# A hybrid decoder layer on one core: stores moved to SyncE's queue, taps and branch pieces traced later

## The chip, the cores and the metric

The kernel runs on one core of a Trainium2 chip. The metric is the time of one execution on the device in microseconds (us), the median of several runs. A core has TensorE (PE in the profile; PEld is its weight load), VectorE (DVE), ScalarE (ACT), GpSimd (POOL) and SyncE (SP). SP, ACT and POOL can each issue DMA transfers; each takes its own instructions, the issues among them, in order, and an instruction that waits holds up what stands behind it on that engine.

## The reference, cut to what matters

One layer over 256 tokens of width 2048, all in float32:

```python
h = rmsnorm(x, pre_norm_g)
q_a, c_kv, k_rope, z_mla, c_in, b_gate, c_gate, z_conv, g_mla, g_conv = split(h @ w_in)
q  = rmsnorm(q_a, q_a_norm_g) @ w_q_b             # 16 heads of 128 + 64 (rotary)
kv = rmsnorm(c_kv, kv_a_norm_g) @ w_kv_b          # 16 heads, keys 128 and values 128
attn = softmax(causal(q k^T * scale)) v * silu(z_mla)
y_mla  = attn @ w_o_mla                            # 2048 x 2048
u = c_gate * c_in
conv = sum(conv_w[k] * shift(u, 2 - k) for k in range(3))
y_conv = (b_gate * conv * silu(z_conv)) @ w_o_conv # 2048 x 2048
merged = sigmoid(g_mla) * y_mla + sigmoid(g_conv) * y_conv
out = x + rmsnorm(merged @ w_out, post_norm_g)
```

## The kernel before

**A product.** PE works in fp32r. Each float32 operand is split into a high part (an ACT copy, `hi`, line 263) and a low part (a DVE subtraction, `lo`, line 264), and a product is three matmuls: high by high, low by high, high by low. Weights come from memory in units of 2048 columns by 128 rows (1 MB): a `raw` tile (three buffers, loaded by SP in `load_raw`, line 165), split by halves into `whi` and `wlo` (five buffers of 1024 columns each). `plan` lists the units in order; `ahead` loads up to three units ahead of use and splits one ahead. A quarter of a 2048 x 2048 product (four blocks of 128 rows, two token halves t = 0 and 1, each into its own PSUM bank) is 24 matmuls of 512 columns. The helper `products` first runs the 16 matmuls with `whi` for both banks and then the 8 with `wlo`; the helper `product` runs the three matmuls of one block one after the other.

**The heads stage** (up to about 608 us). After the two latents, a loop over 16 heads h runs four quarters each, `channels(h, 0..3)`, into two banks `cv` that the next head uses again (one of the four channel projections c_gate, c_in, b_gate, z_conv for a block of 512 columns per head, so four heads make one block of the convolution branch). `channels_done` reads the banks out: ACT lines 804 and 808, DVE lines 806 and 812. At every fourth head four quarters of `gates` (z_mla, banks `z`) come first, with the values of four heads (`group_v`, whose banks `vv` share the tag of `cv`). Between the quarters stand the heads' own small matmuls: `qn`, `kn`, `qr`, scores (`sc`, `sw`), values (`o`). Transposes go over memory: DVE transposes 32 x 32 blocks (line 356), POOL stores (`far<-via`, line 364) and loads them back (line 368).

**Taps.** `taps(j, t)` makes the convolution: POOL brings shifted copies of u into `mv` (line 830) and the filter rows into `cw`, DVE multiplies and adds (line 846). It is a generator in three parts, advanced by `next(tap)` at chosen places of the loop.

**Forms.** The gates g_mla and g_conv are computed by a Strassen-like scheme in seven half-size products, whose left operands are sums of quarters of x, the `FORMS`. `make_forms` builds 14 parts of them in the heads stage (ACT line 894, DVE line 896), two buffers, and POOL stores each to memory (`far_form`, line 901) when the generator is next advanced; SP loads the whole form back later (`bring_form`, line 924).

**The paired stage** (about 608 to 967 us). A sequence `seq` of steps, each with load, split, matmuls and something to run after: four sets s0 to s3 of the scheme (steps Q1, V5, V6, V7, V3, V4, Q2, banks sX, sZ, sY, weights `b`, `first_rt`, `first_rb`, `first_rc`) with the quarters of the two branch products between them (p: attention, four blocks, operand `at_both`; v: convolution, operand `cv_both`; banks `sq`). Splits are traced when the step two places earlier runs. Two of the additions of weights in a set are made by the transfer itself (`add_by_transfer`, POOL, line 1241). `turned_unit` loads transposed operands into a raw buffer and splits them. In s0 and s1 `weigh` multiplies a branch block with its gate and `keep` stores it (`kept_m`, POOL, line 1135). In s2 and s3 `merge` takes it back (`fetch`, line 1138, two buffers `y`), adds the other branch, transposes the sum by DVE and stores it by four POOL transfers (`far_m`, line 364). `later(n, fn)` runs fn n steps later.

**The out stage** (from 967 us). w_out in 16 units, operand `m_both` loaded from `far_m` by POOL; then norm, residual `xr` (2 MB, loaded on ACT's queue, line 1521) and stores.

Instructions marked `keep_in_program_order` stay in the order of tracing on their engine: all matmuls, nearly all DMA issues named here, SP's loads from `u_first` on. Others, most splits and the raw loads of the heads stage among them, are put in order at build time by a planner with a model of the times.

## Time and profile before

| | |
|---|---|
| median of 3 runs | 1063.7 us (1063.62 to 1066.05) |
| the profiled execution's own time | 1066.4 us |
| its span, first to last instruction | 1064.6 us |
| PE busy | 1018.1 us, 4552 matmuls |
| DVE, ACT, POOL busy | 793.2, 579.6, 201.0 us |
| mean granted TensorE clock | 0.984 |

A row of the timeline reads: start, duration, engine, line, operation, tiles written and read, shapes, count, and in brackets the idle time of the engine just before and what ended it. A row of the waits reads: engine, tile and line that waited, the engine and instruction waited for, microseconds in total, number of times, the longest. A row of groups ends with busy time, mean duration and idle time with its releasers.

### The profile page before, as it was taken

To read this page: it belongs to the slowest core of one execution; us is meant where nothing else is said; L and a number is where in the kernel's file an instruction comes from. 1 tells how busy PE (TensorE), PEld (TensorE's weight loads), DVE (VectorE), ACT (ScalarE), POOL (GpSimd) and SP (SyncE) were. 2 spreads that over 40 slices of the span, in tenths; PEclk is the share of its full clock that TensorE was granted. 3 is DMA by queue.
4 is the path that set the end of the run, shared out by engine and by line. 5 is a ranking of instruction groups with operands and counts; after the bars stand their busy time and mean duration, and the time that the engine had idled before them with its cause. 6 is when DMAs were issued, how large, how long until landed. Compare 5 with 4: busy or idle time off the path is not lost.

```text
span 1064.6 us, 13052 instructions
## 1 busy us (share of the span) xinstructions
PE 1018.1 (96%) x4552; PEld 839.3 (79%) x4552; DVE 793.2 (75%) x1087; ACT 579.6 (54%) x824; POOL 201.0 (19%) x362
## 2 busy tenths in 40 slices
PE   9999999999899999999999976999999999799997
PEld 7888788887688778788788755888788788588786
DVE  7588878778667796767868486788788789586562
ACT  7675545655446555455555443664665665473451
POOL 4610322203411223212233120001010013102100
PEclk9999999999899999999999988999999999899999
DMA  9776777768777675856677979989889885949652
GB/s 358 288 239 227 268 241 261 253 207 299 240 274 237 222 269 197 273 201 224 242 255 273 325 259 352 342 309 256 262 324 300 267 322 172 256 185 363 233 187 79
DMA packets 52882, 275.22 MB, mean 259 GB/s; under 512 B 8880, under 2 KB 11568, under 8 KB 26960
## 3 DMA queue, kind: packets, MB, share of 16 engines
q1 hardware_dynamic: 35280, 213.30, 54.8%
q0 software_dynamic: 17104, 57.80, 19.6%
q10 hardware_dynamic: 432, 3.29, 0.8%
q8 instruction: 35, 0.57, 0.2%
q14 instruction: 31, 0.25, 0.1%
HBM read 246.07 MB, written 24.12 MB: 254 GB/s over the span
## 4 chain that ended last, share of the span: by engine, by line
PE 72%; DMA 14%; DVE 7%; ACT 3%; issue 3%; POOL 1%; DVEq 0%; ACTq 0%; SPq 0%; POOLq 0%
PE cv L88 22%; PE sq L88 15%; PE sX L88 7%; PE out L88 6%; PE z L88 6%; PE sZ L88 4%; DMA raw<-wcv_dram 3%; DVE wlo L264 3%; DMA raw<-wsq_dram 2%; PE qa L88 2%; PE sY L88 2%; PE ckv L88 2%; DMA cw<-cwr_dram 2%; DMA far_form<-form 2%; PE kn L88 2%
## 5 line engine op out<-in xcount | busy, mean ns | idle before, releaser
L263 ACT ACTIVATE whi<-raw 128x1024 fp32r<-128x1024 f32 (+1 forms) x302 | 301.0, 1024 | 276.5 <-PE cv L88 95.7
L264 DVE TENSOR_TENSOR wlo<-raw,whi 128x1024 fp32r<-128x1024 f32 (+1 forms) x300 | 350.4, 1189 | 119.9 <-ACT whi L263 52.3
L88 PE MATMUL cv<-whi,x_both 128*128 128x512 f32 x1024 | 246.0, 393 | 7.9 <-ACT cv_f L804 4.3
L88 PEld LDWEIGHTS cv<-whi,x_both 128*128 128x128 f32 x1024 | 191.5, 189 | 51.2 <-ACT cv_f L804 6.0
L88 PE MATMUL cv<-wlo,x_both 128*128 128x512 f32 x512 | 126.4, 389 | 0.0
L88 PEld LDWEIGHTS cv<-wlo,x_both 128*128 128x128 f32 x512 | 96.1, 188 | 19.9
L264 DVE TENSOR_TENSOR slo_V<-b,shi_V 128x1024 fp32r<-128x1024 f32 x60 | 71.5, 1221 | 29.9 <-PE sq L88 14.5
L263 ACT ACTIVATE shi_V<-b 128x1024 fp32r<-128x1024 f32 x60 | 61.5, 1053 | 53.7 <-PE sq L88 34.4
L88 PE MATMUL sq<-whi,at_both 128*128 128x512 f32 x256 | 64.9, 408 | 11.2 <-ACT whi L263 11.2
L364 POOL DMA_DIRECT2D far<-via x64 | 35.3, 557 | 193.5 <-DVE via L356 191.0
L88 PEld LDWEIGHTS sq<-whi,at_both 128*128 128x128 f32 x256 | 50.8, 200 | 23.0 <-ACT whi L263 12.0
L88 PE MATMUL z<-whi,x_both 128*128 128x512 f32 x256 | 60.7, 389 | 0.0
L88 PE MATMUL sq<-whi,cv_both 128*128 128x512 f32 x256 | 60.6, 389 | 0.0
L88 PE MATMUL sX<-shi_V,form 128*128 128x512 f32 x192 | 49.4, 401 | 8.7 <-ACT sb L1282 8.7
L88 PEld LDWEIGHTS sq<-whi,cv_both 128*128 128x128 f32 x256 | 48.1, 188 | 10.0
L88 PEld LDWEIGHTS z<-whi,x_both 128*128 128x128 f32 x256 | 47.8, 188 | 9.9 <-ACT at_f L535 0.2
L88 PE MATMUL out<-whi,m_both 128*128 128x512 f32 x208 | 49.8, 390 | 2.2 <-ACT m_both L263 1.4
L88 PEld LDWEIGHTS sX<-shi_V,form 128*128 128x128 f32 x192 | 36.9, 193 | 17.7 <-ACT sb L1282 10.0
L88 PEld LDWEIGHTS out<-whi,m_both 128*128 128x128 f32 x208 | 39.0, 188 | 11.0 <-ACT m_both L263 1.8
L264 DVE TENSOR_TENSOR slo_Q<-b,shi_Q 128x1024 fp32r<-128x1024 f32 x28 | 33.6, 1221 | 5.4 <-PE sq L88 3.2
L263 ACT ACTIVATE shi_Q<-b 128x1024 fp32r<-128x1024 f32 x28 | 28.7, 1053 | 15.4 <-PE sq L88 7.5
L88 PE MATMUL sq<-wlo,at_both 128*128 128x512 f32 x128 | 32.2, 391 | 0.7 <-DVE wlo L264 0.7
(304 smaller groups left out, 1552.0 us busy)
## 6 DMA issues: line engine op xcount, KB each, us to landing
raw<-wcv_dram SPq DMA_DIRECT2D x64, 1024.0 KB, 5.9
raw<-wsq_dram SPq DMA_DIRECT2D x48, 1024.0 KB, 6.3
b<-wsq_dram SPq DMA_DIRECT2D x26, 1024.0 KB, 8.7
raw<-wz_dram SPq DMA_DIRECT2D x16, 1024.0 KB, 4.9
b<-wsq_dram POOLq DMA_DIRECT2D x12, 1024.0 KB, 11.7
raw<-wqk_dram SPq DMA_DIRECT2D x8, 1024.0 KB, 6.8
far_form<-form POOLq DMA_DIRECT2D x14, 512.0 KB, 8.6
form<-far_form SPq DMA_DIRECT2D x7, 1024.0 KB, 14.4
```

What stands on the lines that cost most here:

```text
L88: return tc.keep_in_program_order(nc.tensor.matmul(*a, **kw))
L263: a = nc.scalar.activation(hi, src, AF.Copy)
L264: b = nc.vector.tensor_tensor(lo, src, hi.bitcast(F32), op=ALU.subtract)
L364: tc.keep_in_program_order(queue.dma_start(out=f[i], in_=m))
```

## The change

- `far_form` (14 stores), `kept_m` (8) and `far_m` (32 in 8 blocks) are issued by SP instead of POOL. In `weigh` and `merge` the store, and in `merge` the next fetch, is traced one step later (`later(1, ...)`); if the block that a merge needs is not on its way, it is fetched at once. Of s3 the last two blocks are fetched at V7 into an area of their own instead of through the two `y` buffers.
- `quarter` (all 80 quarters of the heads stage) uses `product` per block, bank t = 0 first and then bank t = 1.
- At heads 4, 8 and 12 the taps' second part moves from the second to the fourth quarter of `gates`, the third part from before `gates_done` to after `channels(h, 0)`.
- The weights `first_rt` of s0's first step are fetched by SP at quarters 0 and 2 of head 14, form 11 at head 15 instead of 14.
- Each `turned_unit` is split by blocks, one step per block; the first unit of `at` moves from the end of head 15 into s0 behind Q1; the others are spread likewise.
- `xr` is issued by SP, in order behind the raw loads traced before it.

```diff
@@ load_raw
+        elif i in u_first:
+            pieces = []
@@ quarter
-        products([
-            (pss[t][:, :], [x_both[:, k, o + t * P : o + (t + 1) * P] for o in (0, S)], w(k - 4 * i, 512), k == 0, k == KD - 1)
-            for t in range(NT) for k in range(4 * i, 4 * i + 4)
-        ])
+        for t in range(NT):
+            for k4 in range(4):
+                k = 4 * i + k4
+                a = [x_both[:, k, o + t * P : o + (t + 1) * P] for o in (0, S)]
+                product(pss[t][:, :], a, w(k4, 512), k == 0, k == KD - 1)
@@ channels
+        if h == H - 2 and i in (0, 2):
+            u = u_first[i // 2]
+            tc.keep_in_program_order(nc.sync.dma_start(out=early[u][:, :], in_=plan[u][0]))
         if i == 3:
             if h == H - 1:
-                at_u[0][0]()
                 ahead(u_first[0])
-                at_u[0][1]()
@@ make_forms
-                    nc.gpsimd.dma_start(
+                    nc.sync.dma_start(
@@ turned_unit
-        return [load, split, None, None]
+        return [[load if i == 0 else None, split(i), None, None] for i in range(len(far))]
@@ the loop over heads
                 elif v and i == 1:
                     pt = turn(ps_by_head.pop(h - 1))
-                    next(tap)
...
+                elif v and i == 3:
+                    next(tap)
-            if v:
-                next(tap)
-            else:
+            if not v:
                 latent_split("ckv", ckv, "kv_g")
...
         channels(h, 0)
+        if v and at == 0:
+            next(tap)
...
-        if h == H - 2:
+        if h == H - 1:
             bring_form("11")
@@ keep
-        queue = nc.gpsimd if key[0] == "m" else nc.scalar
-        tc.keep_in_program_order(queue.dma_start(out=kept[key][:, :], in_=t[:, :]))
+        tc.keep_in_program_order(nc.sync.dma_start(out=kept[key][:, :], in_=t[:, :]))
@@ weigh
-        keep(("m", c, t), g)
+        later(1, lambda: keep(("m", c, t), g))
@@ merge
+        if (c, t) not in fetched:
+            fetch()
...
-        go, _ = turned(m[:, :], g[:, :], 4, far_m[c][:, 512 * t : 512 * (t + 1)])
-        go()
-        fetch()
+        go, _ = turned(m[:, :], g[:, :], 4, far_m[c][:, 512 * t : 512 * (t + 1)], nc.sync)
+        later(1, go)
+        later(1, fetch)
@@ the sequence
-        "Q1": p[0][:2], "V5": at_u[1:2] + p[0][2:3] + at_u[2:3] + p[0][3:],
+        "Q1": at_u[:1] + p[0][:1] + at_u[1:2] + p[0][1:2], "V5": at_u[2:3] + p[0][2:3] + at_u[3:] + p[0][3:],
...
-    also(s3["V6"][1], lambda: first_fetches([(2, 1), (2, 0), (3, 0), (3, 1)]))
+    also(s3["V6"][1], lambda: first_fetches([(2, 1), (2, 0)]))
+    def last_fetches():
+        area = spool.tile([P, UNIT], F32, name="m3_area", tag="f6", bufs=1)
+        for t in range(NT):
+            fetched[3, t] = area[:, 512 * t : 512 * (t + 1)]
+            again(("m", 3, t), fetched[3, t])
+    also(s3["V7"][1], last_fetches)
@@ the out stage
-    nc.scalar.dma_start(out=xr[:, :, :], in_=x)
+    tc.keep_in_program_order(nc.sync.dma_start(out=xr[:, :, :], in_=x))
```

More of the change, by code (lines that the diff above doesn't have):

```diff
@@ L957, in load, with split, go @@
             box.append(t)
-        def split():
-            for i in range(len(far)):
+        def split(i):
+            def go():
                 for t in range(NT):
@@ L963, in split @@
                     split_turned(box[0][:, o : o + 512], both[first + i], t)
-        return [load, split, None, None]
+            return go
+        return [[load if i == 0 else None, split(i), None, None] for i in range(len(far))]
     def split_turned(src, both, t):
@@ L984, in tile_layer @@
     at_b, cv_b = (Late(n, lambda i, n=n: both_tile(n, i)) for n in ("at", "cv"))
-    at_u = [turned_unit(far_at[a:b], at_b, a) for a, b in ((0, 2), (2, 3), (3, 4))]
-    cv_u = [turned_unit(far_cv[a:b], cv_b, a) for a, b in ((0, 2), (2, 4))]
+    at_u = [u for a, b in ((0, 2), (2, 3), (3, 4)) for u in turned_unit(far_at[a:b], at_b, a)]
+    cv_u = [u for a, b in ((0, 2), (2, 4)) for u in turned_unit(far_cv[a:b], cv_b, a)]
     for h in range(H):
@@ L1362, in also @@
         u[3] = lambda: (old and old(), fn())
-    for u, m in ((s3["V7"][1], 0), (v[3][2], 1)):
-        also(u, m_load[m][0])
-    also(s3["V4"][1], m_load[0][1])
+    for u, m in ((s3["V7"][1], 0), (v[3][3], 1)):
+        also(u, m_load[m][0][0])
+    also(s3["V4"][0], m_load[0][0][1])
+    also(s3["V4"][1], m_load[0][1][1])
     def first_fetches(order):
@@ L1381, in tile_layer @@
     for i, u in enumerate(raw_units):
-        loads.append((at_split(u), at_split(raw_units[i - 3]) + 1 if i > 2 else -1 if i < 2 else 0, u[0]))
+        loads.append((at_split(u), at_split(raw_units[i - 3]) + 1 if i > 2 else -1, u[0]))
     for i in range(len(raw_units), len(raw_units) + 3):
@@ L1422, in tile_layer @@
             seq[j][3]()
+    for n in sorted(pending):
+        for fn in pending.pop(n):
+            fn()
     for l in loads:
@@ L1427, in tile_layer @@
     assert not wanted and not fetched
-    last_m = m_load[2]
+    last_m = m_load[2][0]
     def out_products(pss, w, kk, ts=range(NT)):
@@ L1445, in tile_layer @@
         elif i == 2:
-            m_load[1][1]()
+            m_load[1][0][1]()
         out_products(pss[c], w, kk)
```

2 lines of the change are left out of this document (1 added, 1 removed).

## The prediction, made before the changed kernel was built

> **What bounds the kernel now.** I read the busy shares first, then what PE waited for, then PE's timeline and, at each long wait, the timelines of the other engines.
>
> ```profile
> PE 1018.1 (96%) x4552; PEld 839.3 (79%) x4552; DVE 793.2 (75%) x1087; ACT 579.6 (54%) x824; POOL 201.0 (19%) x362
> ...
> PE sX L88 <- ACT sb L1282: 8.7, 3, 7.2
> ...
> PE cv L88 <- ACT cv_f L804: 4.3, 4, 1.5
> ...
> PE cv L88 <- ACT cv_w L808: 1.2, 2, 0.8
> ```
>
> PE is the bound: 1018.1 of the span's 1064.6 us. The change removes no matmul, so what it can win is PE's idle time, 46.5 us, and the matmuls that run at a lower clock just after its longest waits. I go through the change by the places of these waits: three stand here, the others in the rows below. All sums are made against the profiled execution's own 1066.4 us, which is 2.7 above the median 1063.7.
>
> **The order of matmuls in a quarter.** Does `product` cost PE time? The kernel has both orders: z quarters use `products`, `vv` uses `product`.
>
> ```profile
> 344.31 3.79 PE L88 MATMUL z<-whi,x_both 128*128 128x512 f32 x16
> ...
> 349.75 3.79 PE L88 MATMUL z<-whi,x_both 128*128 128x512 f32 x16
> ...
> 355.42 0.39 PE L88 MATMUL vv<-whi,ckv 128*128 128x512 f32 x1
> ...
> 360.86 0.28 PE L88 MATMUL sc<-kn,qn_hi 128*128 128x256 f32 x1
> ```
>
> From 344.31 to 349.75 are 5.44 us for 24 matmuls; from 355.42 to 360.86, the 24 of `vv`, 5.44 too: 0.227 us each either way, price nothing. What the order moves is when things are needed. Bank t = 0 is finished 12 matmuls (2.7 us) before the quarter's end instead of 4 (0.9 us), so ACT can read it out 1.8 us sooner, and the next head's first 12 matmuls use that bank alone. The waits on `cv_f` and `cv_w` are 4.3 + 1.2 = 5.5 us, the longest 1.5, shorter than 1.8. ACT works in order and may come late to the read-out, so I take -4.5 (bounds 0 and -5.5).
>
> The other side: `wlo` is needed with the second matmul, not the 17th (3.4 us earlier), and `whi` comes free 6 to 8 matmuls (1.4 to 1.8 us) later.
>
> ```profile
> L264 DVE TENSOR_TENSOR wlo<-raw,whi 128x1024 fp32r<-128x1024 f32 x282 | 338.3, 1221 | 119.9 <-ACT whi L263 52.3 <-PE cv L88 33.8 <-PE out L88 16.2
> L263 ACT ACTIVATE whi<-raw 128x1024 fp32r<-128x1024 f32 x282 | 289.2, 1053 | 274.4 <-PE cv L88 95.7 <-DMA raw<-wsq_dram 29.8 <-PE out L88 20.8
> ...
> 235.09 3.79 PE L88 MATMUL cv<-whi,x_both 128*128 128x512 f32 x16
> ...
> 235.84 1.83 DVE L264 TENSOR_TENSOR wlo<-raw,whi 128x1024 fp32r<-128x1024 f32 x2
> ```
>
> ACT's largest wait before a split is for PE to free buffers (95.7 us): splits run ahead. The tightest quarter of the 80 starts at 235.09; its second low half starts at 235.84 and takes 1.22, so it is done 2.0 us after the start, and the new order wants it at the 7th matmul, 1.6 us after: 0.4 late. With buffers freed later I take +1 (0 to +3, the bound being two such quarters late by a buffer's 1.4).
>
> **Taps at head 8, forms at head 6.** Two of PE's waits come from the order on DVE.
>
> ```profile
> 277.96 0.68 DVE L896 TENSOR_TENSOR form<-at_f,form 128x512 fp32r<-128x512 f32 x1
> ...
> 282.29 0.58 PE L88 MATMUL sc<-kn,qn_hi 128*128 128x256 f32 x1 [4.13 <-DVE kn L264]
> ...
> 284.16 5.13 PE L88 MATMUL cv<-whi,x_both 128*128 128x512 f32 x16
> ...
> 367.62 0.69 DVE L846 TENSOR_TENSOR mv<-mv,cw 128x512 f32<-128x512 f32 x1 [4.24 <-DMA cw<-cwr_dram]
> ...
> 370.10 3.92 PE L88 MATMUL cv<-whi,x_both 128*128 128x512 f32 x16 [2.35 <-DVE vv_lo L264]
> ```
>
> At 367.62 DVE stands 4.24 us for a filter row, and `vv_lo`, which frees the bank, stands behind it. Traced two quarters later, the tap's second part falls behind `vv_lo`: -2.3 (0 to -2.4). The tap must now end before the join after quarter 2 of head 8; two quarters, 11 us, hide it. At 277.96 a form part stands ahead of `kn`. It could not be made before a POOL store freed its buffer; with stores on SP the parts can be made earlier and leave this place, and the read-out of bank 0, also in DVE's line there, moves ahead. At stake are 4.13 and, at the low clock, 5.13 - 3.79 = 1.3: bounds 0 and -5.5. I take -3, the middle, since no row shows the new order.
>
> **The handover to the paired stage.**
>
> ```profile
> 595.43 1.29 DVE L264 TENSOR_TENSOR at_both<-turned_at,at_both 128x512 fp32r<-128x512 f32 x2 [3.39 <-ACT at_both L263]
> ...
> 600.26 0.52 POOL L837 MEMSET mv<- 1x512 f32 x1 [9.92 <-DVE cv_f L846]
> ...
> 613.78 0.69 DVE L846 TENSOR_TENSOR mv<-mv,cw 128x512 f32<-128x512 f32 x1 [8.38 <-DMA cw<-cwr_dram]
> ...
> 617.23 0.73 PE L88 MATMUL sX<-wlo,form 128*128 128x512 f32 x2 [3.33 <-DVE wlo L264]
> 621.09 5.69 PE L88 MATMUL sq<-whi,at_both 128*128 128x512 f32 x16 [3.13 <-ACT whi L263]
> ...
> 640.04 0.33 SPq L165 DMA_DIRECT2D raw<-wsq_dram  x1
> ...
> 653.13 2.00 ACT L263 ACTIVATE whi<-raw 128x1024 fp32r<-128x1024 f32 x2 [11.28 <-DMA raw<-wsq_dram]
> ...
> 654.24 6.15 PE L88 MATMUL sq<-whi,at_both 128*128 128x512 f32 x16 [8.04 <-ACT whi L263]
> ...
> 614.00:648.00 34.00, 25.17 (x98) 19.25 (x98) 32.52 (x34) 13.18 (x16) 7.29 (x12) 0.90 0.79 256
> ```
>
> The split of the first `at` unit makes DVE late at 595.43; so the last tap ends late, POOL starts the next tap's loads at 600.26, their rows land for 613.78, and PE waits 3.33 and 3.13 us, with 5.69 - 3.79 = 1.9 at the low clock: 8.4. The change takes that unit out of this place: DVE was free at 595.43 - 3.39 = 592.0, so the chain can start some 6 us earlier. Its four subtractions, 2 x 1.29 = 2.6 us, come back behind Q1, where DVE has no room (32.52 of 34 us busy): -8.4 + 2.6, say -6. The fourth quarter then waits 8.04 and loses 6.15 - 3.79 = 2.4: its load left at 640.04, when the split of another `at` unit had freed the buffer, and landed 13.1 us later. That order stays, so I take -2 of 10.4. Together -8 (0 to -16).
>
> **POOL's queue at the end of s2.**
>
> ```profile
> 886.54 1.09 POOL L364 DMA_DIRECT2D far_m<-sa  x2 [19.12 <-DVE sa L356]
> ...
> 889.00 0.57 POOL L1138 DMA_DIRECT2D m<-kept_m  x1
> ...
> 901.81 2.17 POOL L364 DMA_DIRECT2D far_m<-sc  x4 [10.07 <-DVE sc L356]
> 903.97 2.76 POOL L1241 DMA_DIRECT2D b<-wsq_dram  x3
> ...
> 921.78 3.71 PE L88 MATMUL sX<-shi_V,form 128*128 128x512 f32 x8 [7.20 <-ACT sb L1282]
> ...
> 884.51 18.46 SPq L165 DMA_DIRECT2D raw<-wsq_dram  x4
> ...
> 903.54 3.79 PE L88 MATMUL sq<-whi,cv_both 128*128 128x512 f32 x16
> ...
> raw<-wsq_dram SPq DMA_DIRECT2D x48, 1024.0 KB, 6.3
> raw<-wcv_dram SPq DMA_DIRECT2D x64, 1024.0 KB, 5.9
> ```
>
> POOL stands 10.07 us for a merged block, the adding transfers of V5 leave at 903.97 behind it, ACT stands for them with V7's split, and PE pays 7.20 at 921.78. With the stores gone from POOL they can leave when V5 is split, some 10 us earlier. V6 and V7 meet in s1 and s2 too and wait (8.7 - 7.2)/2 = 0.75 each there; that much stays. Lost at the low clock: 3.71 less half of 3.79, 1.8. So 7.20 - 0.75 + 1.8 = -8.2. But the stores now stand in SP's queue, and behind them the load that went at 884.51, whose quarter starts at 903.54. The store needs the block's transpose; its fetch moves from 889.00 to 886.5, so it can go near 901.8 - 2.5 = 899.3, and the load leaves 14.8 us later than now. It has 903.54 - 884.51 - 6.3 - 1.05 = 11.7 us to spare. The new wait is 3.1 with the median landing, 10 with the 13.1 us of 640.04, none if DVE transposes sooner. I take +5, nearer the median since it is the same queue: net -3 (-8 to +2).
>
> **The rest.**
>
> ```profile
> 967.64 1.13 ACTq L1521 DMA_DIRECT2D xr<-x_dram  x1
> ...
> 990.39 0.50 PE L88 MATMUL out<-whi,m_both 128*128 128x512 f32 x1 [1.39 <-ACT m_both L263]
> 991.73 3.71 PE L88 MATMUL out<-whi,m_both 128*128 128x512 f32 x15 [0.84 <-DVE m_both L264]
> ...
> POOL far_form L901 <- DVE form L896: 45.2, 4, 14.6
> ...
> far_form<-form POOLq DMA_DIRECT2D x14, 512.0 KB, 8.6
> ```
>
> 2 MB of `xr` leave at 967.64, among the raw loads that ACT then stands for ahead of `m_both`. Behind eight raw loads `xr` leaves some 20 us later and is read only by the last norm: 1.39 + 0.84 = -2.2 (0 to -2.2). Costed at nothing: `kept_m` on SP (the loads behind it go up to eight steps ahead), `first_rt` a head earlier and form 11 in its place (PE has no load wait there), smaller split steps. Where such a cover fails, a late load costs what the one above does, 3 to 10 us.
>
> Sum: -4.5 + 1 - 2.3 - 3 - 8 - 3 - 2.2 = -22, so 1044.4 for an execution like the profiled one, 1042 against the median.
>
> **Rivals.** *SP's queue becomes what POOL's was* (slower). Forms too stand ahead of raw loads now. POOL waited four times for a form, 45.2 us, the longest 14.6. A head's raw load has three quarters less landing and two halves on ACT to spare, 3 x 5.44 - 5.9 - 2 x 1.05 = 8.3 us; from a hold of that length on this decides. If SP stood as long, PE would wait 6.3 + 3 x 1.9 + 1.3 of low clock = 13.3, and for the load at 884.51, landing in 13.1 us, 10 + 1.8. These 25.1 stand against -4.5, -2.3, -2.2 and -8.2 and with +1: 1066.4 + 8.9 - 2.7 = 1073. For it: all these loads share one queue. Against it: POOL's waits hold time in which it had nothing else to do, and the planner may put head loads ahead of a store. Chance 0.13. [...]
>
> *The planner keeps DVE's order*, so head 6 and the handover stay as they are: 1042 + 11 = 1053, chance 0.17; DVE's 32.52 of 34 us speak for it. *All of it comes*: -5.5 - 2.4 - 5.5 - 16 - 8 - 2.2 = -39.6, 1024, chance 0.15; the load of 640.04 speaks against it. *The waits move on*: each is paid back at the next split that ACT or DVE has in line, 1064, chance 0.07.
>
> *Stores queue behind loads.* On POOL a form lands in 8.6 us. On SP it starts behind a raw load and may land 5.9 later; the next part of that form, made in the same buffer, is as late, and if one wait of head 6's kind comes of it (5.5), the time is 1047: chance 0.05. [...]
>
> **How the numbers follow.** Likeliest, 0.43: 1042, own range 1033 to 1052. Between 1026 and 1064 lie the likeliest, the kept order, the late forms, most of the no-change case and a part of the best: about 0.8. A measurement of this kernel can tell 0.3%, 3 us, from no change; faster 0.80, same 0.07, slower 0.13.
>
> **What would show it.** Right: no wait of `cv` for `cv_f`; `vv_lo` ahead of the tap's `mv` at head 8; the adding transfers of V5 before 896; at most 1 us idle at V7 of s3; `xr` after 985. Wrong: raw loads of heads 3 to 7 issued just behind a `far_form` store, with ACT waiting for raw; over 8 us before the quarter now at 903.54; the handover's three waits in their places.

## The result, and the profile after

The changed kernel takes 1056.99 us (median of 8 runs, 1052.72 to 1060.09), the kernel before 1065.54 beside it (8 runs): a ratio of 0.9907, 95% interval 0.988 to 0.9935. By the ratio that is 9.9 us faster, by the two medians 8.6, where 22 were forecast. The profiled execution took 1056.64, its span is 1054.9.

PE's line of the page after, and then what PE waited for (us in total, times, longest):

```profile
PE 1016.8 (96%) x4552; PEld 841.3 (80%) x4552; DVE 793.7 (75%) x1087; ACT 583.0 (55%) x824; POOL 170.2 (16%) x308
```
```profile
PE sq L88 <- ACT whi L265: 13.3, 3, 9.8
PE sc L88 <- DVE kn L266: 6.2, 2, 4.6
PE o L88 <- DVE pt L266: 3.2, 1, 3.2
PE sZ L88 <- ACT shi_V L265: 3.0, 1, 3.0
PE sX L88 <- ACT sb L1289: 2.3, 3, 0.8
PE sq L88 <- DVE at_both L266: 2.2, 1, 2.2
PE cv L88 <- ACT cv_w L812: 1.3, 1, 1.3
```

The waits for `cv_f`, `vv_lo` and `m_both` are gone. Those for `kn`, for `pt` and for `whi` have grown, and `shi_V` and `at_both` are new.

The table puts this by place. A place's loss is the time from each matmul's start to the next one's, less 0.227 us for 512 columns (in proportion for fewer: the traces' medians are 0.227, 0.120 and 0.060 for 512, 256 and 128), summed over the place: idle time and the low clock after it together. In the changed kernel the granted clock was 0.63 from 644.96 to 651.2, right after PE's longest wait, and 1.00 from 300 to 320, where PE never waits. It is worked out from all 4552 matmul rows of one trace for each column. Two columns are experiments, told below: *order* is the kernel before with the new order of matmuls alone, *best1* a combination.

| place (us before) | before | after | order | best1 |
|---|---|---|---|---|
| four head boundaries (113, 250, 395, 532) | 5.4 | 0 | 0 | 0 |
| heads 2 and 3 (141, 171) | 0.6 | 3.6 | 0 | 0 |
| head 6, `sc` for `kn` (282) | 6.7 | 7.7 | 4.0 | 2.4 |
| head 8, filter row (361 to 370) | 2.7 | 0 | 3.6 | 3.0 |
| handover (602 to 628) | 10.9 | 7.6 | 2.7 | 2.8 |
| fourth quarter (645 to 659) | 11.1 | 12.2 | 11.9 | 11.8 |
| third cv quarter of s2 (about 814 after) | 0 | 2.5 | 0 | 0 |
| end of s2 (892 to 905 after) | 0 | 7.8 | 0 | 0 |
| V7 of s3 (922) | 9.1 | 1.0 | 9.0 | 1.0 |
| `m_both` (990) | 2.8 | 0 | 6.1 | 0 |
| all of the span | 63.0 | 53.2 | 49.6 | 32.0 |

The whole fell by 9.8 us, as the time did. 19.0 us went from boundaries, head 8, V7 and `m_both`, 3.3 from the handover, and some 3 in pieces of 1.2 or less that the table leaves out; 15.4 came at heads 2, 3 and 6, at 814, at the end of s2 and in the fourth quarter.

One profile is not exact to the last of these. A second profile of the changed kernel loses 4.0 us in the handover (7.6 in the table), 14.7 in the fourth quarter (12.2), 4.0 at 814 (2.5) and 9.8 at the end of s2 (7.8). So a difference of 2 to 4 us at one place between two single profiles shows nothing by itself.

The end of s2 is the largest new loss. Its rows, engine by engine (start, length, engine, line, out<-in, count, and in brackets the idle time before and its releaser):

```profile
879.45 1.78 SPq L366 DMA_DIRECT2D far_m<-sa  x4
895.63 1.75 SPq L366 DMA_DIRECT2D far_m<-sc  x4
897.49 9.63 SPq L167 DMA_DIRECT2D raw<-wsq_dram  x4
...
880.31 1.82 POOL L1248 DMA_DIRECT2D b<-wsq_dram  x2
...
891.05 0.60 ACT L1289 ACTIVATE sa<-sX 128x512 f32<-128x512 f32 x1 [11.16 <-DMA far_m<-sa]
903.31 2.00 ACT L265 ACTIVATE whi<-raw 128x1024 fp32r<-128x1024 f32 x2 [8.83 <-DMA raw<-wsq_dram]
...
892.62 1.23 DVE L266 TENSOR_TENSOR slo_V<-b,shi_V 128x1024 fp32r<-128x1024 f32 x1 [5.29 <-ACT shi_V L265]
894.90 0.70 DVE L358 STREAM_TRANSPOSE sc<-m 128x512 f32<-128x512 f32 x1
...
892.65 2.08 PE L88 MATMUL sZ<-shi_V,form 128*128 128x512 f32 x4 [3.02 <-ACT shi_V L265]
904.42 3.95 PE L88 MATMUL sq<-whi,cv_both 128*128 128x512 f32 x16 [1.37 <-ACT whi L265]
```

It reads as a chain. The four stores of the sa block leave SP from 879.45; ACT, which is to write that tile next, stands 11.16 us until the last of them has landed; PE then waits 3.02 for the split behind it, and with the low clock after it (0.58 from 892.65 to 900) loses 6.1. DVE, held by ACT, transposes the sc block only at 894.90; SP, which has stood for it, stores it at 895.63 and sends the raw load behind it at 897.49; ACT gets that at 903.31, and PE waits again, 1.7 lost. So there are two things that I had foreseen as one: a store that lands late, and a store that holds SP's line.

### The profile page after: what moved, and what is told of

Read it like the earlier page. It is cut to its first block, busy times and chain, and to the rows that moved or that the text cites. A ratio compares the mean times of both kernels' runs of the same rounds, so it can differ in the third digit from the quotient of the medians.

```text
span 1054.9 us, 12990 instructions
## 1 busy us (share of the span) xinstructions
PE 1016.8 (96%) x4552; PEld 841.3 (80%) x4552; DVE 793.7 (75%) x1087; ACT 583.0 (55%) x824; POOL 170.2 (16%) x308
## 4 chain that ended last, share of the span: by engine, by line
PE 76%; DMA 12%; DVE 6%; ACT 2%; issue 2%; POOL 1%; SPq 1%; DVEq 0%; ACTq 0%; POOLq 0%
PE cv L88 24%; PE sq L88 12%; PE out L88 8%; PE z L88 8%; PE sX L88 7%; DMA raw<-wsq_dram 4%; PE sZ L88 3%; PE qa L88 2%; PE sY L88 2%; PE ckv L88 2%; DVE wlo L266 2%; PE vv L88 2%; PE qn L88 2%; PE kn L88 2%; DMA raw<-wcv_dram 2%
## 5 line engine op out<-in xcount | busy, mean ns | idle before, releaser
L265 ACT ACTIVATE whi<-raw 128x1024 fp32r<-128x1024 f32 (+1 forms) x302 | 305.1, 1027 | 246.8 <-PE cv L88 82.4
L88 PE MATMUL cv<-whi,x_both 128*128 128x512 f32 x1024 | 321.6, 391 | 1.3 <-ACT cv_w L812 1.3
L88 PE MATMUL cv<-wlo,x_both 128*128 128x512 f32 x512 | 200.2, 391 | 0.0
L88 PE MATMUL z<-whi,x_both 128*128 128x512 f32 x256 | 80.0, 389 | 0.0
L88 PE MATMUL z<-wlo,x_both 128*128 128x512 f32 x128 | 49.8, 389 | 0.0
L88 PEld LDWEIGHTS sX<-shi_V,form 128*128 128x128 f32 x192 | 35.8, 188 | 10.9 <-ACT sb L1289 3.6
L1248 POOL DMA_DIRECT2D b<-wsq_dram x12 | 10.4, 895 | 189.2 <-ACT whi L265 97.1
```

What stands on the lines that cost most here:

```text
L88: return tc.keep_in_program_order(nc.tensor.matmul(*a, **kw))
L265: a = nc.scalar.activation(hi, src, AF.Copy)
L1248: tc.keep_in_program_order(nc.gpsimd.dma_start(out=dst[:, :], in_=wsq[n, c + b, k], accum_op=ALU.add))
```

## The experiments

A ratio is to the kernel before, run beside it on the same chip. Edits are to the changed kernel unless said otherwise.

### The order of matmuls alone, and everything but it

To the kernel before:

```diff
-        products([... for t in range(NT) for k in range(4 * i, 4 * i + 4)])
+        for t in range(NT):
+            for k4 in range(4):
+                ...
+                product(pss[t][:, :], a, w(k4, 512), k == 0, k == KD - 1)
```

> The kernel before with one edit: a quarter's matmuls are issued bank by bank with the low-half product right behind its high-half one, as in the changed kernel; queues, taps, forms and split steps stay as before. Theory (the order is what took the waits for the bank's read-out at the head boundaries): the four places where cv waited for cv_f, 1.43 + 1.78 + 1.11 + 1.11 = 5.4 us of PE's loss, go, and nothing comes in their place: about 5 us faster than before, ratio 0.995. Rival 1 (those waits went with the stores, which left DVE and POOL in another order): they stay, ratio 1.000. Rival 2 (the earlier need of the low half costs as much, through late splits): new waits of PE for wlo of 3 us or more inside quarters, ratio 0.998 to 1.002.

> The changed kernel once more, as the yardstick for the three beside it: 0.988 to 0.9935 of before.

Measured: 1050.87 us, ratio 0.9845 (0.9806 to 0.9884), 16 us faster than before by the ratio and 14 by the medians; the changed kernel beside it 1057.48, 0.9912 (0.9883 to 0.9941). The order alone is worth more than the whole change. The four boundaries went, as the theory said, but that is 5.4 of 13.4 us of loss. 8.2 came from the handover and 2.7 from head 6, which no theory had named. The rows of this kernel:

```profile
584.55 0.69 DVE L847 TENSOR_TENSOR cv_f<-cv_f,mv 128x512 f32<-128x512 f32 x1
586.64 1.29 DVE L264 TENSOR_TENSOR at_both<-turned_at,at_both 128x512 fp32r<-128x512 f32 x2 [1.40 <-ACT at_both L263]
...
585.30 0.52 POOL L838 MEMSET mv<- 1x512 f32 x1 [5.05 <-DVE cv_f L847]
...
885.17 2.17 POOL L364 DMA_DIRECT2D far_m<-sc  x4 [10.08 <-DVE sc L356]
```

Before, the last product of that tap stood on DVE behind the split of `at_both` (595.43) and POOL could start the next tap at 600.26. Here DVE's list has the two the other way round, and POOL starts at 585.30. That is 15 us earlier, of which PE itself was 9.4 ahead (its last head's first quarter starts at 574.9, before at 584.3), so the chain gained some 6. The split unit has not moved: the matmuls' order is the only edit, so it is the planner that wrote another order for DVE. The last row shows POOL's hold for the sc block as it was.

And the reverse, the changed kernel with the old order:

> The changed kernel with one edit: a quarter's matmuls in the order of the kernel before (all high halves of a bank, then the low ones); everything else as changed. The order alone took 16 us from the kernel before (ratio 0.9845), the whole change 9 to 10. Theory (the other parts cost more than they bring, and the order's gain stands beside them): without the order the changed kernel is 1.003 to 1.010 of before, 4 to 8 us slower, with the read-out waits of 5 us back at the head boundaries. Rival (the other parts bring something of their own, and parts overlap with the order's gain): 0.995 to 1.000.

Measured: 1067.59 us, ratio 1.0004 (0.998 to 1.0027). All the other parts together bring nothing: their gains and costs cancel. That is better than my theory (4 to 8 us slower), and the 5 us that it wanted back at the head boundaries did not come: this profile loses 1.5 there. So the order is enough to take those waits away, but most of them go by the other parts too.

### Who pays for the sc block's store

```diff
-        go, _ = turned(m[:, :], g[:, :], 4, far_m[c][...], nc.sync)
-        later(1, go)
+        go, _ = turned(m[:, :], g[:, :], 4, far_m[c][...], QUEUE)
+        later(N, go)
```

with QUEUE and N: all on POOL, 1 (*merge_pool*); t = 0 (sa, sb) on POOL and t = 1 (sd, sc) on SP, 1 (*merge_x*); sc alone on POOL, 1 (*merge_y*); all on POOL, N = 4 for sc and 1 for the others (*merge_late*).

> The changed kernel with the merged blocks' stores back on POOL's queue, still traced one step behind. In the changed kernel PE loses 7.8 us between 892 and 905 us; ACT stands 11.2 us there for the store of the sa block to land. Theory A (the store is issued with two adding transfers of 1 MB leaving beside it on the other queue, and lands late; ACT, then DVE's transpose of the sc block, then SP's next store and the raw load behind it are late in turn): on POOL the store leaves ahead of the adding transfers, the 7.8 us go, the loss at V7 of the fourth set stays at 1.0 since the sc store now stands behind the adding transfers in POOL's line: 6 to 8 us faster than the changed kernel, about 0.984 of before. Theory B (the store must leave ahead of the adding transfers and they wait for it, as in the kernel before): the 7.8 go but the 8.1 at V7 come back, no gain. Theory C (bandwidth alone: 892 to 905 is short of landed loads whatever the queue): losses of 6 us or more stay there.

> The changed kernel with the merged blocks' stores split over two queues: the first row half (sa, sb) on POOL, ahead of the adding transfers, the second (sd, sc) on SP. With all of them on POOL the loss at 892 to 905 us (9.8 in the same set's run of the changed kernel) went, and 7.6 us came back at V7, where the adding transfers stood 5.6 us for the sc store. Theory A (the late landing of the sa store in ACT's line is what starts the 892 to 905 loss; SP's hold for sc follows from it): both losses go, at most 2 us stay in the two places together, sa waits under 2 us for its store; 7 to 9 us faster than the changed kernel. Theory B (SP's hold for the sc block costs by itself, since a raw load stands behind it): ACT's wait goes, but PE still waits 3 us or more for whi near that place.

> The other way round: sa, sb and sd stores on SP as in the changed kernel, the last (sc) on POOL. Theory A: the sa store again lands 10 us or more after issue, ACT stands for it, and the wait of sZ for shi_V (3.0 to 3.6 us) stays; the raw load no longer stands behind sc, so the wait of sq for whi 12 us later shrinks from 1.4 or more towards 0. Theory B: both waits go, since SP has nothing to stand for.

> The changed kernel with all merged blocks' stores on POOL, and the sc block's traced four steps behind instead of one, so that in POOL's line it stands behind the adding transfers of V5 and in SP's line nothing stands for it. So far: all on SP loses 8 to 10 us at 889 to 908 us, sa and sb on POOL with sc on SP 9.0 there (a raw load leaves at 891.6 behind the sc store), sc on POOL ahead of the adding transfers 8.6 to 9.2 at V7. Theory (the loss belongs to whatever stands in line behind the store that waits for DVE's transpose of sc, at about 890 us): with nothing urgent behind it both places lose at most 2 us together, 7 us less than the changed kernel, about 0.984 of before. Rival (bandwidth: the raw loads and the adding transfers of that stretch cannot all land in time): 5 us or more stay at one of the two.

| | ratio (interval) | loss at the end of s2 | loss at V7 of s3 |
|---|---|---|---|
| changed kernel, beside the first | 0.9912 (0.9883 to 0.9941) | 9.8 | 1.0 |
| merge_pool | 0.9886 (0.9858 to 0.9914) | 0 | 8.6 |
| merge_x | 0.9895 (0.9872 to 0.9917) | 9.0 | 1.0 |
| merge_y | one run, 1057.54 us | 0 | 9.2 |
| merge_late | 0.9826 (0.980 to 0.9851) | 0 | 1.0 |

In merge_pool it came as theory B says: the new loss goes and the one at V7 comes back. In merge_x ACT no longer stands for the sa store, and yet nothing is gained:

```profile
889.56 1.93 SPq L366 DMA_DIRECT2D far_m<-sc  x4
891.59 13.37 SPq L167 DMA_DIRECT2D raw<-wsq_dram  x4
...
884.54 0.58 ACT L1289 ACTIVATE sa<-sX 128x512 f32<-128x512 f32 x1
901.15 2.00 ACT L265 ACTIVATE whi<-raw 128x1024 fp32r<-128x1024 f32 x2 [13.84 <-DMA raw<-wsq_dram]
```

`sa` is written at 884.54 with no wait for its store, so the late landing was a cost of the changed kernel, but not the one that decides. The raw load still leaves behind the sc store, at 891.59, and lands 9.6 us later. In merge_y it is the adding transfers' turn:

```profile
891.07 2.20 POOL L366 DMA_DIRECT2D far_m<-sc  x4 [10.26 <-DVE sc L358]
893.33 1.82 POOL L1248 DMA_DIRECT2D b<-wsq_dram  x2
...
884.17 0.60 ACT L1289 ACTIVATE sa<-sX 128x512 f32<-128x512 f32 x1 [3.73 <-DMA far_m<-sa]
```

Theory A is wrong in merge_x, where it wanted both losses gone and 7 to 9 us, and theory B held in all three. The loss of 8 to 9 us belongs to whatever stands in line behind the store that waits for DVE. That was the theory of merge_late, and it held: put behind the adding transfers, the store holds nothing up.

```profile
880.41 1.82 POOL L1248 DMA_DIRECT2D b<-wsq_dram  x2 [2.15 <-issue]
883.86 2.24 POOL L366 DMA_DIRECT2D far_m<-sc  x4 [1.63 <-DVE sc L358]
...
871.03 18.47 SPq L167 DMA_DIRECT2D raw<-wsq_dram  x4
```

The adding transfers leave at 880.41, the raw loads from 871.03, and DVE, not held up, has the sc block ready for 883.86. Bandwidth, the rival, is not the bound there: the same loads and stores are issued in all five kernels, and here neither place loses.

### The form stores

*forms_pool* has the form stores back on POOL; *forms_three* leaves them on SP and gives the parts three buffers:

```diff
-                f = early_pool.tile([...], F32R, name=..., tag="form", bufs=2)
+                f = early_pool.tile([...], F32R, name=..., tag="form", bufs=3)
```

> The changed kernel with the form stores back on POOL's queue. In the changed kernel PE waits for kn at head 6 (7.7 us lost, 6.65 before), at head 2 (2.0, 0.6 before) and for cv_w at head 3 (1.6, 0.1 before); ACT stands 13.5 us in all, eight times, for a form store to land before it can write the form's buffer again. Theory (on SP a store is issued behind a raw load of 1 MB and lands 7 us after issue, and kn's high half stands in ACT's line behind the form part that waits): on POOL the waits at heads 2 and 3 shrink to the sizes before (0.6 and 0.1), head 6 loses about 6.65 as before; 3 to 4 us faster than the changed kernel. Rival (the places of the form parts among the splits are what costs, whichever queue stores them): head 6 loses 6 to 8 again and heads 2 and 3 keep 2.0 and 1.6; no change.

> The changed kernel with three buffers for the form parts and not two; their stores stay on SP. ACT stands 13.5 us there, in eight waits, for a store to land before it writes a form part, and kn's or a raw split's high half stands behind it. Theory (the landing of the stores is what costs, through the buffer): ACT's waits for far_form fall under 2 us, and the losses at heads 2, 3 and 6 (2.0, 1.6, 7.7) to about 0.5, 0.1 and 2 to 4: 4 to 7 us faster than the changed kernel, about 0.986 of before. Rival (the stores in SP's line hold the raw loads, or the parts' places cost): the losses stay.

> The fastest kernel so far (order, late sc store, residual last; 0.971 of before) with one part of the change added: form stores on SP's queue. Theory: 2 to 5 us slower than without (0.973 to 0.976), by waits for kn at heads 2 and 6 and for cv_w at head 3. Rival (the stores on POOL cost as much in another way): no difference, 0.971.

Measured: forms_pool 0.9887 (0.986 to 0.9913), 1053.73 us, 3.8 below the changed kernel beside it; losses 0.4 at head 2, none at head 3, 4.0 at head 6 (7.2 in the run beside it). best1_forms_sp 0.9747 (0.9715 to 0.9779) against 0.9711 (0.9689 to 0.9733) without: heads 2 and 6 lose 3.8 and 8.0, against 0 and 2.4. So form stores on SP cost 3 to 4 us in both kernels by the medians, though in each pair the intervals overlap. Head 6 bears it out over many profiles. Ten others of the changed kernel and of its variants give every engine the same list up to there: nine lose 7 to 10 us and one, merge_late's, loses 2.2 (its profiled execution was its fastest, 1042.13 where the median is 1048.09). The five with the new order and form stores on POOL lose 2.4 to 4.2. The changed kernel's rows at head 6:

```profile
272.43 0.33 SPq L167 DMA_DIRECT2D raw<-wqr_dram  x1
272.81 0.97 SPq L905 DMA_DIRECT2D far_form<-form  x1
...
279.63 0.63 ACT L898 ACTIVATE form<-cv_f 128x512 fp32r<-128x512 f32 x1 [3.33 <-DMA far_form<-form]
280.16 0.40 ACT L265 ACTIVATE kn<-f 128x256 fp32r<-128x256 f32 x1
...
281.70 0.58 PE L88 MATMUL sc<-kn,qn_hi 128*128 128x256 f32 x1 [4.56 <-DVE kn L266]
```

The store leaves just behind a raw load, ACT waits 3.33 us for it before it may write the buffer again, and `kn` stands behind that in ACT's line. The landing is not slower than on POOL: the median form store lands 8.0 us after its issue here and 8.6 before. What changed is which part stands there. The parts are made earlier, as the prediction said: the ninth, which DVE made at 277.96 before, ahead of `kn`, is now made 41 us sooner. But the eleventh has come into its place (DVE writes it at 280.29, behind ACT's 279.63):

```profile
237.28 0.69 DVE L900 TENSOR_TENSOR form<-at_f,form 128x512 fp32r<-128x512 f32 x1
```

forms_three should have taken the wait for the buffer away. It did at head 2 (no loss), but head 3 kept 1.5, head 6 lost 7.5, and the ratio stayed at 0.9902 (0.9868 to 0.9936). ACT no longer waits there for a form, and DVE waits for something else:

```profile
274.81 0.43 DVE L745 TENSOR_TENSOR at_f<-f,at_f 128x256 f32<-128x256 f32 x1 [4.39 <-issue]
...
268.07 0.57 POOL L370 DMA_DIRECT2D at_f<-far  x1 [4.27 <-DMA far<-cw]
275.02 0.55 POOL L366 DMA_DIRECT2D far<-via  x1 [2.57 <-DMA at_f<-far]
```

The profile names no releaser for DVE, but the tile that it reads was loaded by POOL at 268.07 and landed at 274.73, and POOL's next store waits for the same landing. So at head 6 a second wait lies close behind the first. That the stores' queue costs there is shown; by which way is not, and this stays open.

### The moved unit in the handover

```diff
+                at_u[0][0]()
                 ahead(u_first[0])
+                at_u[0][1]()
+                at_u[1][1]()
...
-        "Q1": at_u[:1] + p[0][:1] + at_u[1:2] + p[0][1:2],
+        "Q1": p[0][:2],
```

> The changed kernel with the first turned unit of the attention output loaded and split at the last head, as before, and not behind Q1 of the paired stage. The changed kernel loses 4.1 to 7.6 us between 592 and 616 us and 12 to 15 at the fourth quarter (about 645); with the new order alone, which keeps the old place, it is 2.7 and 11.9. Theory (the change's move of this unit costs here, and the gain foreseen for it came from the order of matmuls, which made DVE finish the taps earlier): 2 to 3.5 and 11 to 12, about 3 to 5 us faster than the changed kernel, about 0.988 of before. Rival (the moved unit is what helps and the later taps or DVE's order cost): the first rises towards the 10.9 of before, no gain or a loss.

Measured: 1050.56 us, ratio 0.9861 (0.9824 to 0.9897), against 0.9907 (0.988 to 0.9935) for the changed kernel: some 5 us, with the intervals just overlapping. Handover 5.7, fourth quarter 9.4, together 15.1 where the changed kernel's two profiles lose 18.7 to 19.8. The parts did not come as forecast (2 to 3.5 and 11 to 12), the sum did. Nine profiles of the changed kernel and its variants, with the same lists up to here, lose 17 to 22 us in the two places together, so 15.1 lies below all of them. The move costs and does not help. The changed kernel's rows (the last one, of a stretch: its ends, its length, busy us and number of instructions of PE, PEld, DVE, ACT and POOL, the granted clock, the share of time that the DMA engines are busy, GB/s):

```profile
595.97 0.69 DVE L850 TENSOR_TENSOR mv<-mv,cw 128x512 f32<-128x512 f32 x1 [5.23 <-DMA cw<-cwr_dram]
...
603.06 0.47 PE L88 MATMUL o<-pt,vv_hi 128*128 128x512 f32 x1 [3.19 <-DVE pt L266]
...
611.74 5.28 PE L88 MATMUL sq<-whi,at_both 128*128 128x512 f32 x15 [2.17 <-DVE at_both L266]
644.96 6.08 PE L88 MATMUL sq<-whi,at_both 128*128 128x512 f32 x16 [9.81 <-ACT whi L265]
...
611.00:667.00 56.00, 45.46 (x183) 36.93 (x184) 41.23 (x37) 25.98 (x29) 7.00 (x11) 0.88 0.98 315
```

DVE still stands for a filter row, 5.23 us, with `pt` behind it; the moved split is now itself what PE waits for at 611.74; and from 611 to 667 the DMA engines are busy 0.98 of the time. The raw load that the fourth quarter waits for left at 628.21 and landed 15.5 us later; in at_back, without the moved unit's load in this stretch, it took 12.9 from 627.00. At 644.96, at a granted clock of 0.63, sixteen matmuls take 6.08 us instead of 3.79.

Does the move start the chain earlier? Counted from the start of the last head's first quarter on PE, POOL starts the last tap after 16.0 us before, 10.4 with the order alone, 9.2 in order_back (old order, the unit moved), 7.8 in the changed kernel and 7.5 in at_back. So the order alone starts it 6 us earlier and the other parts without it 7, and with both the move adds nothing.

### The new loss at about 814 us

> The changed kernel with the two halves of each turned unit of two blocks split at one step, as before, and not one block later. The changed kernel loses 2.5 to 4.0 us at 813 us (0 before): the raw load there left at 801.0, when the second half of the turned unit had been split and freed the ring's buffer, and landed 11.7 us later. Theory (the halved steps hold the ring's buffer 5 us longer): that loss goes to under 0.5; the wait for at_both in the handover (2.2 us) may change either way; the fourth quarter there, 12 to 15 lost, does not change, since its load waits for another unit. About 2 to 4 us faster than the changed kernel. Rival (the load is late by bandwidth alone, the engines being full in that stretch): the 2.5 stay.

> The changed kernel with the weighed blocks' stores (kept_m) on POOL as before, still a step behind. In the changed kernel PE loses 2.5 to 4 us at 812 to 816 us; SP stands 8.9 us there for the weighed sa block, and the turned units and raw loads behind it leave 787 to 801. Theory (SP's hold for that store is the cause, since splitting the turned units in one step did not help): the loss goes to under 0.5. Rival (the engines are full in that stretch, the load lands late anyway): 2 us or more stay.

> The changed kernel with two parts undone together: the weighed blocks' stores on POOL, and the turned units of the second branch split in one step. Each alone left a loss of 3.0 and 8.4 us at about 810 us, where the changed kernel has 2.5 to 4 and the kernel before none. Theory (both lengthen the hold of the raw ring's buffers there; only together undone the loads leave as early as before): under 1 us at 805 to 816. Rival (the loss comes of loads that are issued earlier elsewhere in the stretch and fill the engines): 2 us or more stay.

split_whole puts the two halves of a turned unit at one step again (`cv_u[:2] + v[0][:2]`), keep_back the weighed blocks' stores on POOL, cv_keep does both for the second branch. Measured: split_whole 0.9888 (0.9856 to 0.992), 3.0 us lost at 810; keep_back 1060.65 us in one run, 8.4 lost there; cv_keep 1055.35 in one run, nothing lost there. In split_whole and keep_back PE's wait is another one: it stands 2.0 and 5.4 us for `slo_V`, since DVE stands 3.3 and 8.4 for the load of its weights `b`. Both theories of a single cause fell, and the joint one held in its one profile. Its reason, that the loads then leave earlier, is not borne out: the raw load that the quarter needs left at 793.57 in the changed kernel and at 793.85 in cv_keep, and landed at 812.65 and 810.31. Why the two parts together cost 2.5 to 4 us there stays open.

### The residual

> The changed kernel with the residual's load back on ACT's queue, placed by the planner. The changed kernel loses nothing at the first output products that read m_both; before it was 2.8, and with the new order alone 6.1. Theory (the 2 MB of the residual among the raw loads are what ACT's splits, and m_both behind them, come late for): 2.5 to 6 us are lost there again, 0.993 to 0.996 of before. Rival (the earlier merged blocks and smaller split steps took that wait): under 0.5 there, 0.991.

Measured: 1062.58 us, ratio 0.996 (0.9937 to 0.9983), and 6.5 us lost at the matmuls that read `m_both` again, where PE waits 3.93 for `whi`. Its ACT rows:

```profile
959.94 1.35 ACTq L1540 DMA_DIRECT2D xr<-x_dram  x1
...
972.65 1.16 ACT L265 ACTIVATE m_both<-turned_m 128x512 fp32r<-128x512 f32 x2 [9.30 <-DMA turned_m<-far_m]
978.68 2.00 ACT L265 ACTIVATE whi<-raw 128x1024 fp32r<-128x1024 f32 x2 [4.87 <-DMA raw<-wsq_dram]
```

The 2 MB leave at 959.94; the turned block that is needed next lands for 972.65, and the raw load for 978.68. In the changed kernel the same two wait 5.21 us for the block and for no raw load:

```profile
969.25 1.15 ACT L265 ACTIVATE m_both<-turned_m 128x512 fp32r<-128x512 f32 x2 [5.21 <-DMA turned_m<-far_m]
974.75 2.01 ACT L265 ACTIVATE whi<-raw 128x1024 fp32r<-128x1024 f32 x2 [4.35 <-PE out L88]
```

### What is left when only the gains are kept

The kernel before with the new order, the sc store four steps behind on POOL, and the residual last on SP's queue (best1); with the later taps too (best2); best1 with the loads of the stored forms three steps ahead and not eight (best3).

> The kernel before with the new order of matmuls, the sc block's store four steps behind on POOL, and the residual loaded last on SP's queue; forms, taps and split steps as before. The order alone ran at 0.9845 of before and its profile still lost 9.0 us at V7 of the fourth set and 6.1 at m_both (ACT stood for raw loads while the residual's 2 MB came in). Theory: both go, leaving 1 us each: 13 us less, 0.972 of before, about 1038. Rival (the loads of the last stretches are late by bandwidth, so the losses move to the next split): 0.980 or more.

> The same with the taps traced later at a gate stretch, as in the changed kernel. With the order alone PE loses 3.6 us at head 8, where DVE stands for a filter row ahead of vv_lo; in the changed kernel nothing. Theory: that loss goes and nothing else moves: 3 us less than without the later taps, about 0.969 of before. Rival (the planner makes another order elsewhere, as it did with the matmuls' order): the 3.6 go, and 2 us or more come at other heads or in the handover.

> The fastest kernel so far with the loads of the stored forms issued three steps ahead of their use and not eight. In every kernel PE loses 11 to 15 us at the fourth quarter of the paired stage, where the raw load takes 13 us or more to land while all the DMA engines are busy from about 610 to 670 us; 3 MB of forms that are needed later are loaded beside it. Theory (bandwidth: what is loaded early there delays what is needed first): the loss of 11.8 falls by 3 to 7 us, 0.966 to 0.968 of before. Rival (the load's late start sets it, since it waits for the split that frees its buffer): 10 us or more stay, 0.971. The forms may also come late themselves: a new wait of sX or sZ for a form.

Measured: best1 1035.63 us, 0.9711 (0.9689 to 0.9733); best2 1035.89, 0.971 (0.9681 to 0.974); best3 1034.71, 0.9703 (0.967 to 0.9735). All three are 3% faster than before and 2% faster than the changed kernel, and not told apart. In best2 the 3.0 at head 8 go and 1.3, 0.8 and 1.6 us come at other heads; but the same three come in best3, whose lists in the heads stage are those of best1, so they are not the later taps' doing, and neither theory nor rival is shown. In best3 the fourth quarter loses 7.3 for 11.2, but PE waits 2.3 for `slo_V` just ahead of it, 2.6 lost, so the two places together lose 9.9 for 11.8. The raw load there was no faster, 14.0 us from issue to landing for 13.2: that bandwidth goes to the forms instead is not shown, and what sets that wait stays open. best1's line of the page, and PE's longest waits in it:

```profile
PE 1009.5 (98%) x4552; PEld 836.8 (81%) x4552; DVE 792.8 (77%) x1087; ACT 584.2 (57%) x824; POOL 200.8 (19%) x362
```
```profile
PE sq L88 <- ACT whi L263: 8.2, 1, 8.2
PE cv L88 <- DVE vv_lo L264: 2.6, 1, 2.6
PE sX L88 <- ACT sb L1283: 2.3, 3, 0.8
```

PE is busy 1009.5 us here and 1016.8 in the changed kernel, for the same 4552 matmuls, at a mean granted clock of 0.994 against 0.986: fewer long waits are followed by fewer matmuls at the low clock. From 640 to 650 us the changed kernel, with its wait of 9.81, had a clock of 0.52; best1, whose PE is busy all that time, had 1.00. One wait of 8.2 us, the fourth quarter's, is the largest that remains.

## Why the prediction was right or wrong

The direction held. The size did not: 9.9 of 22 us, less than half. 1057 us lies inside the wide range (1026 to 1064) and outside the likeliest case's own (1033 to 1052). It comes near the rival *The planner keeps DVE's order* (1053), whose effect it had, with little gained at head 6 and in the handover, but not its mechanism: DVE's lists did change. Two steps failed by most, the forms (7.1 us short of the forecast) and the handover (5.8). The end of s2 (2.7) and 814 (2.5) follow; the other steps brought 5.9 more than their terms, so 12.2 of the forecast's 22 were missing. By its steps, in us of PE's loss unless said otherwise:

- *Order of matmuls, -4.5 and +1.* The mechanism and its size at the boundaries were right: -5.4, the bound, and PE's waits of `cv` for `wlo` with the order alone come to 0.5 in all. But the step was sized as if an edit moved only its own instructions. Alone it gave -13.4, with 8.2 from the handover, where the planner had given DVE another order, and 2.7 from head 6.
- *Taps at head 8, -2.3.* Measured -2.7, by another way than the one foreseen. `vv_lo` does not stand ahead of the tap's product; it still follows it. But DVE comes to that product only at 361.21, when the filter row has landed (357.11), and stands for nothing:

```profile
361.21 1.29 DVE L850 TENSOR_TENSOR mv<-mv,cw 128x512 f32<-128x512 f32 x2
...
364.08 0.68 DVE L266 TENSOR_TENSOR vv_lo<-vv,vv_hi 128x512 fp32r<-128x512 f32 x1
```

  Before, the row landed at 367.49, and DVE had stood for it. The number is right in part by luck.
- *Forms at head 6, -3.* Wrong sign: +1.1 there and +3.0 at heads 2 and 3. The failed sentence is that with stores on SP "the parts can be made earlier and leave this place". The first half came true, by 41 us; what failed is that the place stays empty. The eleventh part came into it, and ACT, with `kn` behind it, waits 3.33 for that part's buffer. The rival *Stores queue behind loads* (5.5 us, chance 0.05) has this effect in part, a wait of head 6's kind, but not its reason: stores behind a raw load land no later (8.0 us, 8.6 on POOL). forms_three shows the buffer to be the cause at head 2; at head 6 the cause stays open.
- *Handover, -8.* Measured -2.2 in the first profile (10.9 to 7.6, 11.1 to 12.2). The chain did start earlier, by 8 us where "some 6 us" were foreseen, but with the new order it does so without the move as well. The failed step is the price of the unit where it now stands, "Its four subtractions, 2 x 1.29 = 2.6 us" of DVE time: undoing the move is worth about 5 us. I left out that PE would wait for that split itself (2.17) and that the fourth quarter's load would take longer beside the unit's load (15.5 us, 12.9 without), so the -2 for that quarter became +1.1.
- *POOL's queue at the end of s2, -3.* The gain was -8.1 at V7 (foreseen -8.2). The new loss was +7.8 where I took +5, inside its bound of 10, but only 1.7 of it stands before the quarter that was to wait; 6.1 stand before it, by ACT's wait for the sa store, which the term did not have. merge_x, without that wait, shows the foreseen one alone: 9.0, since the load behind the store took 9.6 us to land and not the median's 6.3.
- *Residual, -2.2.* Measured -2.8, and 5.6 us of time when it alone is undone.
- *Costed at nothing.* Form 11 and the first quarters cost nothing to be seen. `kept_m` on SP with the smaller split steps cost 2.5 at 814; undone together it goes, in one profile. I had looked at each edit's cover alone.

Of what was to show it, no wait for `cv_f`, the adding transfers at 880.31 (before 896) and 0.8 us idle at V7 came as said. `vv_lo` ahead of the tap's product did not come, and the residual left at 982.03, not after 985. Of the signs for wrong, form stores do not stand ahead of raw loads: twelve of the fourteen leave within 0.9 us behind one. The 8 us before the quarter of 903.54 came as 7.8 in two places, and of the handover's three waits the fourth quarter's stayed, while waits for `pt` and `at_both` came for the other two.

Three merge rows show what stands behind a waiting store: whichever queue had the sc store, the transfer that was traced behind it left 1.9 to 2.3 us after it (897.49 after 895.63 in the changed kernel and 891.59 after 889.56 in merge_x, on SP; 893.33 after 891.07 in merge_y, on POOL).

## What to carry to other kernels

When a transfer must wait for a late producer, moving it to another queue can move the loss to whatever stands behind it there (here 9.1 us at V7 with the store on POOL, 7.8 at the end of s2 with it on SP); what removed the loss here was to issue it behind the last urgent transfer of its queue (merge_late: 0 and 1.0). Where a planner orders the engines' lists, no edit is local: time every part of a change alone on the old kernel, since one part can carry all of the gain and the rest take some of it back. And when an edit lets a chain of pieces run earlier, ask which piece then stands at the tight place: here the ninth form left it and the eleventh came.

## What the runs showed of the hardware

At the end of s2 small stores that were issued behind adding transfers landed only after one of those had landed, though they were on another queue. In the changed kernel two adding transfers of 1 MB left POOL at 880.31 and 880.91 and landed at 889.21 and 894.39. Of SP's stores of 64 KB, the first three of the sa block, issued from 879.45 to 880.29, landed after 1.7 to 2.9 us. The fourth, issued at 880.80, landed at 890.87, and the four of the sb block, issued from 881.33 to 883.40, between 894.56 and 895.09. The four of the sc block, issued from 895.63 on, took 1.7 to 3.6 us again. The medians (block, number, KB each, us from issue to landing):

```profile
far_m<-sb SPq DMA_DIRECT2D x4, 64.0 KB, 12.8
far_m<-sc SPq DMA_DIRECT2D x4, 64.0 KB, 1.8
```

In merge_x the sc stores, on SP, were issued from 889.56 to 891.01 while an adding transfer was on its way until 897.99; they landed from 898.16 to 898.68. In merge_y no adding transfer left before 893.33, and the eight stores issued from 880.00 to 883.35 landed after 1.7 to 3.0 us. Elsewhere one store went otherwise: of the changed kernel's `kept_m` stores of 256 KB, the one issued at 784.50, 0.1 us behind an adding transfer, landed at 786.51, while those of 785.09 and 786.83 landed at 793.70 and 794.26, after the transfer itself (793.53). Whether the adding itself or the bytes ahead is the reason was not tried.
